# One level of Strassen's scheme in the FFN's first product: seven block products for eight, with the block sums made on the chip

## The chip, the core and the metric

The kernel runs on one core of a Trainium2 chip. Its time is the device time of one execution in microseconds (us). The engines are TensorE (PE; PEld is its weight load), VectorE (DVE), ScalarE (ACT), GpSimd (POOL) and SyncE (SP), whose queue issues nearly all transfers.

## The reference

One step of a backbone of two layers on 640 tokens (512 latent, 128 context) of 1024 features, in fp32. Each layer is an FFN, a mixer of three head groups, and an FFN again. Vectors that shift, scale and gate (`sh`, `sc`, `gt`) come from a conditioning vector by a product with `w_ada`, one set for the context and one for the latent tokens.

```python
def swiglu(x, w_in, w_out):          # w_in 1024 x 5632, w_out 2816 x 1024
    g, u = jnp.split(x @ w_in, 2, axis=-1)
    return (jax.nn.silu(g) * u) @ w_out
...
    u = rmsnorm(h, p["g_norm"][0]) * (1.0 + sc1) + sh1
    h = h + 0.5 * gt1 * swiglu(u, p["w_ff_in"][0], p["w_ff_out"][0])
    u = rmsnorm(h, p["g_norm"][1]) * (1.0 + sc2) + sh2
    y, cache = mix(u, p, lam_init, ctx)
    h = h + gt2 * y
    u = rmsnorm(h, p["g_norm"][2]) * (1.0 + sc3) + sh3
    h = h + 0.5 * gt3 * swiglu(u, p["w_ff_in"][1], p["w_ff_out"][1])
```

## The kernel before

Features lie on the partitions and tokens along them. The tokens are cut into two halves, `HALF`: 384 and 256. An fp32 product is made of three fp32r ones (`mm3`): each operand is a pair H + L, where ScalarE casts H (`split`, L187) and VectorE subtracts it from the fp32 value to give L (L188).

An FFN (`ffn`) has 22 chunks f of 128 hidden features, in three groups of 8, 7 and 7. For each chunk `load1` loads the gate columns and the up columns of `w_ff_in`, 1024 x 128 each, and splits both. `unit1(f, hf)` then multiplies them with the tokens of one half: 2 x 8 x 3 = 48 matmuls into the PSUM tile `gu`. Behind it come tanh on ScalarE and three instructions on VectorE, which give silu(g) * u as a pair for the second product. After a group, `unit2(d, hf)` multiplies all its chunks with 128 columns of `w_ff_out` (PSUM tile `w`), and `update` adds the gated result to the residual `h` on VectorE (L689). `tail` runs the next norm's first half beside the last `unit2` of the second half of the tokens.

The modulation vectors are 72 units, of which 8 are computed in the startup on TensorE. `pump` computes the other 64, one behind each chunk and one behind each column block of the second product, in program order: 32 in the first FFN and 32 in the second, both of layer 0. A unit (`ada_unit`) is a load of 1 MB and 16 multiply-adds of 256 columns on VectorE (`adacc`, L274 and L276), four transposes on TensorE (`adt`) and a reduction (`adred`).

The order of the instructions on each engine is set at build time, from the program order and a model of the engines; on the chip each engine takes its queue in that order. In the startup and in the mixer a planner in the kernel (`Sched`) writes the order, with estimated lengths and due times. The buffers of the FFN's modulation are given back before the mixer begins.

Of the kernel before, what the change touches and what calls it, by code (L numbers as in the profile page):

```python
# [16 lines left out]
P = 128  # L17
D = 1024
# [10 lines left out]
GROUPS = ((0, 8), (8, 15), (15, 22))  # L29
# [5 lines left out]
class Buf:  # L35
    """a buffer of one of the scheduler's pools, held from the operation that allocates it to the last of its users"""
# [9 lines left out]
class Sched:  # L46
    """List scheduler for the mixer: operations with engine, length (ns), dependencies, buffers and deadline (us) are issued in
    the order in which a model of the engines would start them."""
# [33 lines left out]
    def op(self, eng, ns, fn, deps=(), dl=0.0, alloc=(), use=()):  # L82
        """eng: one letter, or several with a length each"""
# [82 lines left out]
class Net:  # L166
    def __init__(self, tc, a, depth=DEPTH):
        self.tc, self.nc, self.a, self.depth = tc, tc.nc, a, depth
        self.n1 = self.n2 = 0
        self.head = None  # L170

# [1 line left out]
    def mm(self, out, lhsT, rhs, start, stop):  # L173
        self.nc.tensor.matmul(out, lhsT, rhs, start=start, stop=stop)  # L174

    def mm3(self, out, sH, sL, mH, mL, start, stop):
        self.mm(out, sH, mH, start, False)
        self.mm(out, sH, mL, False, False)
        self.mm(out, sL, mH, False, stop)

    def split(self, raw, shape):
        """raw (fp32 AP) -> exact fp32r pair"""
        nc = self.nc
        n = int(np.prod(shape[1:]))
        H = self.hlp.tile(shape, F32R, tag="wH", name="wH", bufs=5)
        L = self.hlp.tile(shape, F32R, tag="wL", name="wL", bufs=5)
        nc.scalar.copy(H, raw)  # L187
        nc.vector.tensor_tensor(L, raw, H.bitcast(F32), ALU.subtract)  # L188
        return H, L

# [10 lines left out]
    def rpow(self, out, x):  # L201
        """out = x ** -0.5 (both small fp32 SBUF)"""
# [5 lines left out]
    def consts(self, ctx):  # L208
# [24 lines left out]
            # silu of the conditioning vectors  # L233
# [6 lines left out]
    def mixconsts(self):  # L240
# [5 lines left out]
        # additive masks for the diagonal blocks, [s, t]: fwd keeps s <= t, bwd keeps s >= t  # L246
# [4 lines left out]
        # one-hot columns: a column broadcast over 128 selects a row  # L251
# [47 lines left out]
    def startup(self):  # L299
        """the first modulation vectors, the residual stream to feature-major, its first norm, and the first units of the first FFN"""  # L300
# [1777 lines left out]
```

## Time and profile before

| | |
|---|---|
| median of 3 runs | 2793.17 us (2791.73 to 2793.29) |
| profiled execution | span 2790.0 us from first to last instruction, one core |
| TensorE busy | 2739.9 us, 98% of the span |
| VectorE busy | 1762.5 us, 63% |
| ScalarE busy | 1028.0 us, 37% |
| FFN 1, 2 (layer 0), us from the span's start | 52 to 527, 947 to 1434 |
| FFN 3, 4 (layer 1) | 1434 to 1885, 2312 to 2772 |

Busy is the time in which an engine works on an instruction. Two instructions that overlap on an engine are counted once in its busy time, so the distance between starts, and not the length of one, is what an instruction costs in a row of them. The bounds of the FFNs are read from the chain and rounded.

### The profile page before, as it was taken

Reading aid. Unit: us, or ns where it says so; the run is one execution under the profiler, and the core shown is the slowest. Engines: PE = TensorE matmul, PEld = TensorE weight load, DVE = VectorE, ACT = ScalarE, POOL = GpSimd, SP = SyncE. Lnnn points to the kernel's source line nnn. Section 1 sums busy time; section 2 is a strip of 40 time slices with the busy share of each in tenths; the row PEclk is TensorE's granted clock in tenths of the full one; section 3 lists DMA queues with packets and bytes.
Section 4 is the critical chain, followed back from the end, with each engine's and each line's share of the span. In section 5 each row is a group of like instructions: output and inputs, shape, how many; then the busy total and the mean of one; then the engine's idle time right before and its main releaser. Section 6 shows DMA issues by size and latency. Waiting matters only on the chain.

```text
span 2790.0 us, 46051 instructions
## 1 busy us (share of the span) xinstructions
PE 2739.9 (98%) x18423; PEld 2630.1 (94%) x18423; DVE 1762.5 (63%) x3848; ACT 1028.0 (37%) x2275; POOL 308.8 (11%) x508
## 2 busy tenths in 40 slices
PE   8999999999989999999999999999999999999998
PEld 5999999988889999999999999998888899999998
DVE  5988888666865798788863333338667646333334
ACT  5212222456666421222242122226657644212121
POOL 1000000142522100000000000003343220000000
PEclk9999999999999999999999999999999999999999
DMA  8544454222102354445422222222211033222321
GB/s 264 174 153 142 137 158 134 87 93 88 40 3 77 112 171 137 149 146 152 129 76 76 76 72 80 67 98 81 86 54 31 3 106 83 84 64 69 87 70 52
DMA packets 361933, 276.38 MB, mean 99 GB/s; under 512 B 23720, under 2 KB 349432, under 8 KB 361720
## 3 DMA queue, kind: packets, MB, share of 16 engines
q1 hardware_dynamic: 361720, 273.44, 32.2%
q8 instruction: 145, 2.38, 0.4%
q14 instruction: 68, 0.56, 0.1%
HBM read 259.25 MB, written 14.16 MB: 98 GB/s over the span
## 4 chain that ended last, share of the span: by engine, by line
PE 91%; DVE 3%; ACT 2%; POOL 1%; DMA 1%; issue 1%; SPq 0%; POOLq 0%; DVEq 0%; ACTq 0%
PE gu L174 44%; PE w L174 22%; PE zps L174 6%; PE wo L174 4%; PE tr L965 4%; PE y L174 3%; PE sc L174 2%; PE num L174 2%; PE adt L278 1%; PE z L174 1%; DMA out_new_b_n<-cst 1%; POOL m L1011 1%; PE adp L174 1%; PE st L174 1%; POOL rr L205 0%
## 5 line engine op out<-in xcount | busy, mean ns | idle before, releaser
L174 PE MATMUL gu<-uH,wH 128*128 128x256 f32 (+1 forms) x2816 | 872.4, 310 | 0.0
L174 PE MATMUL gu<-uL,wH 128*128 128x256 f32 (+1 forms) x2816 | 868.9, 309 | 0.1
L174 PE MATMUL gu<-uH,wL 128*128 128x256 f32 (+1 forms) x2816 | 868.6, 309 | 0.0
L174 PEld LDWEIGHTS gu<-uL,wH 128*128 128x128 f32 x2816 | 534.0, 190 | 0.8 <-DVE uL L650 0.4
L174 PEld LDWEIGHTS gu<-uH,wH 128*128 128x128 f32 x2816 | 533.8, 190 | 0.5 <-issue 0.4
L174 PEld LDWEIGHTS gu<-uH,wL 128*128 128x128 f32 x2816 | 533.9, 190 | 0.0
L187 ACT CAST wH<-raw 128x1024 fp32r<-128x1024 f32 (+1 forms) x268 | 274.0, 1022 | 556.7 <-PE w L174 359.1
L174 PE MATMUL w<-hH,wH 128*128 128x384 f32 (+1 forms) x1408 | 435.6, 309 | 0.0
L174 PE MATMUL w<-hH,wL 128*128 128x384 f32 (+1 forms) x1408 | 433.6, 308 | 0.0
L174 PE MATMUL w<-hL,wH 128*128 128x384 f32 (+1 forms) x1408 | 433.0, 308 | 0.0
L188 DVE TENSOR_TENSOR wL<-raw,wH 128x1024 fp32r<-128x1024 f32 (+1 forms) x268 | 319.3, 1193 | 160.1 <-ACT wH L187 159.9
L276 DVE SCALAR_TENSOR_TENSOR adacc<-adaw,cs,adacc 128x256 f32<-128x256 f32 x896 | 385.5, 477 | 2.8
L174 PEld LDWEIGHTS w<-hL,wH 128*128 128x128 f32 x1408 | 264.8, 188 | 0.0
L174 PEld LDWEIGHTS w<-hH,wL 128*128 128x128 f32 x1408 | 264.5, 188 | 0.0
L174 PEld LDWEIGHTS w<-hH,wH 128*128 128x128 f32 x1408 | 264.2, 188 | 0.2 <-DVE o L667 0.2
L689 DVE SCALAR_TENSOR_TENSOR h<-w,mod,h 128x128 f32<-128x128 f32 (+1 forms) x288 | 117.6, 435 | 215.8 <-PE w L174 215.7
L716 ACT ACTIVATE th<-gu 128x256 f32<-128x256 f32 (+1 forms) x173 | 75.2, 434 | 457.5 <-PE gu L174 457.5
L611 POOL TENSOR_TENSOR ssum<-ssum,sq 128x384 f32<-128x384 f32 (+1 forms) x36 | 33.4, 929 | 1899.9 <-ACT sq L610 1886.7
L717 DVE SCALAR_TENSOR_TENSOR th<-th,gu 128x256 f32<-128x256 f32 (+1 forms) x173 | 83.5, 483 | 212.7 <-ACT th L716 212.1
L722 ACT CAST hH<-th 128x256 fp32r<-128x256 f32 (+1 forms) x173 | 79.5, 459 | 251.0 <-DVE th L718 251.0
L174 PE MATMUL zps<-wH,uH 128*128 128x512 f32 x352 | 145.8, 414 | 0.0
L174 PE MATMUL zps<-wH,uL 128*128 128x512 f32 x352 | 139.1, 395 | 0.0
(293 smaller groups left out, 3922.8 us busy)
## 6 DMA issues: line engine op xcount, KB each, us to landing
raw<-in_w_ff_in SPq DMA_DIRECT2D x176, 512.0 KB
adaw<-in_w_ada SPq DMA_DIRECT2D x72, 1024.0 KB
raw<-in_w_ff_out SPq DMA_DIRECT2D x32, 896.0 KB
raw<-in_w_ff_out SPq DMA_DIRECT2D x16, 1024.0 KB
rawi<-in_w_in SPq DMA_DIRECT2D x16, 1024.0 KB
rawo<-in_w_out SPq DMA_DIRECT2D x8, 1024.0 KB
bspill<-z SPq DMA_DIRECT2D x20, 256.0 KB
rawi<-in_w_in SPq DMA_DIRECT2D x8, 512.0 KB
```

What stands on the lines that cost most here:

```text
L174: self.nc.tensor.matmul(out, lhsT, rhs, start=start, stop=stop)
L187: nc.scalar.copy(H, raw)
L188: nc.vector.tensor_tensor(L, raw, H.bitcast(F32), ALU.subtract)
L276: nc.vector.scalar_tensor_tensor(acc, raw[:, k, :], self.cs[:, 8 * v + k : 8 * v + k + 1], acc, ALU.mult, ALU.add)
L278: nc.tensor.transpose(pt[:, (2 * v + j) * P : (2 * v + j + 1) * P], acc[:, j * P : (j + 1) * P], self.ident)
L611: (nc.gpsimd if d in SSG else nc.vector).tensor_tensor(ssum[:, :w], ssum[:, :w], sq[:, :w], ALU.add)
L689: nc.vector.scalar_tensor_tensor(hh, ps[:, s0:s1], gm[:, v, d : d + 1], hh, ALU.mult, ALU.add)
L716: nc.scalar.activation(th[:, :w], ps[:, 0, :w], AF.Tanh, scale=0.5)
L717: nc.vector.scalar_tensor_tensor(th[:, :w], th[:, :w], 1.0, ps[:, 0, :w], ALU.add, ALU.mult)
L722: nc.scalar.copy(H, th[:, :w])
L965: nc.tensor.transpose(pt[:, i * P : (i + 1) * P], x, ident)
L1011: nc.gpsimd.tensor_tensor(m2[:, :, e * hw : (e + 1) * hw], z[:, :, o * hw : (o + 1) * hw], tb[:, 1, e * hw : (e + 1) * hw].unsqueeze(1).to ...
```

## The change

For each chunk the first product is C = A B, where A has two row blocks (gate and up, index s) and two column blocks (the halves of the 1024 features, e), and B has the two halves of the features and two halves of the tokens, now of 320 each (`UH`). Winograd's form of Strassen's scheme makes C of seven block products. On the token side T1 = B12 - B11, T3 = B22 - B12, T2 = B22 - T1 and T4 = B21 - T2 (signs folded into the weights) are made once in each norm (`u_steps`) and held as pairs. On the weight side S1 to S4 are made for each chunk, in the loaded tile, and the seven blocks are split by `split4`. The sums of the products are made partly in PSUM, by going on with an accumulation, and partly on VectorE (`wino`). The last product, which completes the gate of the second token half, is left to the next chunk's pass (`rest`). The first two chunks of an FFN are still computed in the plain way with the new halves (`plain0`, `plain1`).

The groups are four, of 6, 6, 5 and 5 chunks; the second product keeps the old halves and its code otherwise. `pump` is called at the same places: with four groups that makes 36 units in the first FFN and 28 in the second. A modulation unit loads its weights in two halves of 512 KB. In the startup, weights of the modulation have three buffers for five, and GpSimd may make some of the sums; elsewhere `u_steps` runs them on VectorE. Buffers are laid out anew, and four weight pairs are kept for five. The rest of the diff is renaming of buffers and removal of comments.

```diff
-GROUPS = ((0, 8), (8, 15), (15, 22))
+UH = 320
+QK = KD // 2
+GROUPS = ((0, 6), (6, 12), (12, 17), (17, 22))
+UCOMB = dict(B11=(8, 9), B21=(10, 11), B22=(0, 1), T1=(2, 3), T2=(4, 13), T3=(5, 6), T4=(7, 12))
...
+    def split4(self, raw):
+        nc = self.nc
+        i = self.nw8 = (self.nw8 + 1) % 8
+        w = self.wtile("HL"[i % 2], [P, 2, QK, P], i // 2)
+        nc.scalar.copy(w[:, 0], raw)
+        nc.vector.tensor_tensor(w[:, 1], raw, w[:, 0].bitcast(F32), ALU.subtract)
+        return w[:, 0], w[:, 1]
...
+    def ada_unit(self, l, s, u):
         nc, a = self.nc, self.a
         pt = self.ps1("adt")
+        c0 = s * D + u * 256
+        acc = [self.adp.tile([P, 256], F32, tag="adacc", name="adacc", bufs=3) for v in range(2)]
+        for e in range(2):
+            raw = self.adp.tile([P, QK, 256], F32, tag="adaw", name="adaw", bufs=2)
+            nc.sync.dma_start(raw, a["w_ada"][l, e * 512 : (e + 1) * 512, c0 : c0 + 256].rearrange("(k p) c -> p k c", p=P))
+            for v in range(2):
+                for k in range(QK):
+                    col = self.cs[:, 8 * v + 4 * e + k : 8 * v + 4 * e + k + 1]
+                    if e == 0 and k == 0:
+                        nc.vector.tensor_scalar(acc[v], raw[:, 0, :], col, None, ALU.mult)
+                    else:
+                        nc.vector.scalar_tensor_tensor(acc[v], raw[:, k, :], col, acc[v], ALU.mult, ALU.add)
...
-        S = Sched(dict(ps1=4, ps2=2, adaw=5, row=2, nx=2, nu=2, dg=3, w=5, raw=2), strict=("nx", "nu", "dg", "w", "raw"))
+        S = Sched(dict(ps1=4, ps2=2, adaw=3, row=2, nx=2, dg=3, w=4, raw=2), strict=("nx", "dg", "raw"))
...
+    def plain0(self, st, kk, k):
+        B = self.uc["B21" if kk else "B11"]
+        for s in range(2):
+            H, L = st["W"][s]
+            kw = QK * kk + k
+            self.mm3(st["ps"][:, s, :UH], H[:, kw], L[:, kw], B[0][:, k], B[1][:, k], kw == 0, k == QK - 1, True)
...
+    def plain1(self, st, k):
+        T1, B22 = self.uc["T1"], self.uc["B22"]
+        for s in range(2):
+            H, L = st["W"][s]
+            out = st["ps1"][:, s, :UH]
+            self.mm3(out, H[:, k], L[:, k], T1[0][:, k], T1[1][:, k], k == 0, False)
+            self.mm3(out, H[:, QK + k], L[:, QK + k], B22[0][:, k], B22[1][:, k], False, k == QK - 1)
...
+        def t2():
+            th = st["th", hf]
+            nc.vector.scalar_tensor_tensor(th, th, 1.0, g, ALU.add, ALU.mult)
+            nc.vector.tensor_tensor(th, th, u, ALU.mult)
...
+        def xu(d, raw):
+            def x(e):
+                xs[d] = self.npool.tile([P, UH], F32, tag="nx", name="nx", bufs=2)
+                nc.vector.tensor_tensor(xs[d], self.h[d][:, hf * UH : hf * UH + UH], rb, ALU.mult)
+            def u(e):
+                am, bm = self.mod[(l, 3 * i + 1)], self.mod[(l, 3 * i)]
+                r = raw()
+                for v, s0, s1 in segs:
+                    if v == 1 and dve:
+                        nc.vector.tensor_scalar(r[:, s0:s1], xs[d][:, s0:s1], am[:, v, d : d + 1], bm[:, v, d : d + 1], ALU.mult, ALU.add)
+                    else:
+                        nc.scalar.activation(r[:, s0:s1], xs[d][:, s0:s1], AF.Identity, scale=am[:, v, d : d + 1], bias=bm[:, v, d : d + 1])
+            add(("x", d), "D", UH, x)
+            add(("u", d), "A", UH, u, ("x", d))
...
+        def hi(n, k, src, *deps):
+            add(("H" + n, k), "A", UH, lambda e: nc.scalar.copy(uc[n][0][:, k], src()), *deps)
+        def low(n, k, src, *deps):
+            def f(e):
+                if uc[n][1] is None:
+                    self.ut[13] = uc[n][1] = self.utile(13).rearrange("p (k t) -> p k t", k=QK)
+                ve(e).tensor_tensor(uc[n][1][:, k], src(), uc[n][0][:, k].bitcast(F32), ALU.subtract)
+            add(("L" + n, k), "DG", UH, f, *deps)
+        def comb(n, k, dst, a, b, op, *deps):
+            add((n, k), "DG", UH, lambda e: ve(e).tensor_tensor(dst(), a(), b(), op), *deps)
...
+            a, b = (lambda k=k: A[k]), (lambda k=k: B[k])
+            b1, b2 = (lambda k=k: b11[:, k]), (lambda k=k: b21[:, k])
+            xu(k, lambda k=k: new(A, "ua", k))
+            xu(QK + k, lambda k=k: new(B, "ub", k))
+            hi("B22", k, b, ("u", QK + k))
+            low("B22", k, b, ("HB22", k))
+            comb("t3", k, b, b, a, ALU.subtract, ("u", k), ("LB22", k))
+            comb("t1", k, a, a, b1, ALU.subtract, ("t3", k))
+            hi("T1", k, a, ("t1", k))
+            low("T1", k, a, ("HT1", k))
+            hi("T3", k, b, ("t3", k))
+            low("T3", k, b, ("HT3", k))
+            comb("t2", k, b1, b, b1, ALU.add, ("t1", k))
+            comb("t4", k, b2, b2, b1, ALU.subtract, ("t2", k))
+        for k in range(QK):
+            hi("T4", k, lambda k=k: b21[:, k], ("t4", k))
+            low("T4", k, lambda k=k: b21[:, k], ("HT4", k))
+            hi("T2", k, lambda k=k: b11[:, k], ("t2", k))
+        for k in range(QK):
+            low("T2", k, lambda k=k: b11[:, k], ("HT2", k), *(("LT4", z) for z in range(QK)))
...
+            for key, engs, n, fn, deps in self.u_steps(l, i, hf, pb[:, :UH], True, lambda n, k: abt[n][:, k]):
+                fn(engs[0])
...
+        def prod(out, w, name, start):
+            H, L = w
+            uH, uL = self.uc[name]
+            for k in range(QK):
+                self.mm3(out, H[:, k], L[:, k], uH[:, k], uL[:, k], start and k == 0, k == QK - 1, True)
+        def weights(f):
+            raw = load1(f)
+            A11, A12, A21, A22 = (raw[:, s, e * QK : (e + 1) * QK] for s in range(2) for e in range(2))
+            tt = nc.vector.tensor_tensor
+            w = {}
+            w["A11"] = self.split4(A11)
+            tt(A11, A11, A21, ALU.subtract)
+            w["S3"] = self.split4(A11)
+            w["A12"] = self.split4(A12)
+            tt(A11, A22, A11, ALU.subtract)
+            w["S2"] = self.split4(A11)
+            tt(A12, A12, A11, ALU.subtract)
+            w["A22"] = self.split4(A22)
+            tt(A21, A21, A22, ALU.add)
+            w["S1"] = self.split4(A21)
+            w["S4"] = self.split4(A12)
+            return w
+        def rest(st):
+            ps = st["xp"]
+            prod(ps[:, 0, :UH], st["w"]["S4"], "B22", False)
+            st["m"] = (ps[:, 0, :UH], st["m7"])
+            post(st, 1)
+        def wino(f, prev):
+            st = dict(q=f - g0)
+            sc = lambda t, b: self.npool.tile([P, UH], F32, tag=t, name=t, bufs=b)
+            w = st["w"] = weights(f)
+            tt = nc.vector.tensor_tensor
+            xp = st["xp"] = self.ps2("gu")
+            x, p = xp[:, 0, :UH], xp[:, 1, :UH]
+            prod(x, w["A11"], "B11", True)
+            m1 = sc("m1", 1)
+            nc.scalar.copy(m1, x)
+            prod(p, w["S3"], "T3", True)
+            m7 = st["m7"] = sc("m7", 2)
+            nc.scalar.copy(m7, p)
+            if prev is not None:
+                rest(prev)
+            a = self.ps1("ga")[:, :UH]
+            prod(a, w["A12"], "B21", True)
+            tt(m1, m1, a, ALU.add)
+            prod(x, w["S2"], "T2", False)
+            X = sc("X", 1)
+            nc.scalar.copy(X, x)
+            prod(p, w["A22"], "T4", False)
+            tt(X, X, p, ALU.add)
+            st["ps"] = None
+            prod(x, w["S1"], "T1", False)
+            tt(m7, m7, x, ALU.add)
+            st["first"] = (m1, X)
+            post(st, 0)
+            return st
...
+                            if kk == 0:
+                                pl[f]["ps"] = self.ps2("gu")
+                            elif f == 1:
+                                next(self.pend)
+                            for k in range(QK):
...
+            prev = None
             for f in fs:
-                load1(f)
-                for hf in range(2):
-                    unit1(f, hf)
+                prev = wino(f, prev)
                 self.pump(1)
+            rest(prev)
...
-        S.grow("wo", 5)
+        S.grow("wo", 4)
```

## Rows read from the trace of the kernel before

**Rows 1.** The page, part 1: busy us, share of the span, instructions.

```profile
PE 2739.9 (98%) x18423; PEld 2630.1 (94%) x18423; DVE 1762.5 (63%) x3848; ACT 1028.0 (37%) x2275; POOL 308.8 (11%) x508
```

**Rows 2.** The page, part 2: busy tenths in 40 slices.

```profile
PE   8999999999989999999999999999999999999998
...
DVE  5988888666865798788863333338667646333334
```

**Rows 3.** The page, part 4: the chain, by line.

```profile
PE gu L174 44%; PE w L174 22%; PE zps L174 6%; PE wo L174 4%; PE tr L965 4%; PE y L174 3%; PE sc L174 2%; PE num L174 2%; PE adt L278 1%; PE z L174 1%; DMA out_new_b_n<-cst 1%; POOL m L1011 1%; PE adp L174 1%; PE st L174 1%; POOL rr L205 0%
```

**Rows 4.** Windows: the four FFNs; then the start and four passes of FFN 1.

```profile
core 0: us, PE busy (x) PEld busy (x) DVE busy (x) ACT busy (x) POOL busy (x), PEclk, DMA share, GB/s
52.00:527.00 475.00, 475.00 (x3282) 474.82 (x3283) 389.62 (x889) 119.61 (x190) 7.05 (x8) 1.00 0.48 147
947.00:1434.00 487.00, 486.92 (x3360) 486.25 (x3359) 400.08 (x911) 133.79 (x217) 7.00 (x8) 1.00 0.44 135
1434.00:1885.00 451.00, 451.00 (x3083) 451.00 (x3083) 178.39 (x298) 114.61 (x182) 5.53 (x6) 1.00 0.27 80
2312.00:2772.00 460.00, 460.00 (x3142) 459.87 (x3141) 183.16 (x311) 119.22 (x192) 6.13 (x7) 1.00 0.24 69
...
52.00:94.00 42.00, 42.00 (x292) 41.82 (x292) 36.28 (x91) 16.69 (x33) 0.74 (x1) 1.00 0.52 144
108.50:166.50 58.00, 58.00 (x402) 58.00 (x401) 50.69 (x115) 15.32 (x25) 0.00 (x0) 1.00 0.53 168
```

**Rows 5.** Windows, instructions of tile adacc alone: FFN 1, 2 and 3.

```profile
core 0: us, PE busy (x) PEld busy (x) DVE busy (x), PEclk, DMA share, GB/s
52.00:527.00 475.00, 19.39 (x128) 14.67 (x128) 212.28 (x512) 1.00 0.48 147
947.00:1434.00 487.00, 19.34 (x128) 14.67 (x128) 202.04 (x488) 1.00 0.44 135
1434.00:1885.00 451.00, 0.00 (x0) 0.00 (x0) 0.00 (x0) 1.00 0.27 80
```

**Rows 6.** The chain in order of time (start, us, what): passes, second product.

```profile
137.53 14.07 PE gu L174 x96
152.03 14.07 PE gu L174 x96
...
1541.02 55.90 PE w L174 x384
1596.92 98.52 PE gu L174 x672
```

**Rows 7.** Timeline of VectorE, FFN 1 (start, us, instruction, [idle before]).

```profile
start us, us, engine line op out<-in xcount [idle before <-releaser]
...
217.80 2.35 DVE L188 TENSOR_TENSOR wL<-raw,wH 128x1024 fp32r<-128x1024 f32 x2
220.97 0.62 DVE L689 SCALAR_TENSOR_TENSOR h<-w,mod,h 128x384 f32<-128x384 f32 x1 [0.82 <-PE w L174]
223.80 0.61 DVE L689 SCALAR_TENSOR_TENSOR h<-w,mod,h 128x128 f32<-128x128 f32 x2 [2.21 <-PE w L174]
224.32 0.68 DVE L280 TENSOR_REDUCE adred<-adt 128x4 f32<-128x512 f32 x1
...
225.52 5.62 DVE L276 SCALAR_TENSOR_TENSOR adacc<-adaw,cs,adacc 128x256 f32<-128x256 f32 x14
231.06 1.22 DVE L188 TENSOR_TENSOR wL<-raw,wH 128x1024 fp32r<-128x1024 f32 x1
```

**Rows 8.** Timeline of VectorE at the head of FFN 3.

```profile
1425.43 1.01 DVE L650 TENSOR_TENSOR uL<-nu,uH 128x384 fp32r<-128x384 f32 x2
...
1427.30 0.56 DVE L650 TENSOR_TENSOR uL<-nu,uH 128x384 fp32r<-128x384 f32 x1
...
1439.37 0.42 DVE L640 TENSOR_TENSOR nx<-h,nbc 128x256 f32<-128x256 f32 x1 [0.51 <-PE nbc L174]
...
1440.17 0.34 DVE L644 TENSOR_SCALAR nu<-nx,mod,mod 128x128 f32<-128x128 f32 x1
1440.43 0.75 DVE L640 TENSOR_TENSOR nx<-h,nbc 128x256 f32<-128x256 f32 x2
...
1441.42 0.60 DVE L644 TENSOR_SCALAR nu<-nx,mod,mod 128x128 f32<-128x128 f32 x2
```

**Rows 9.** Groups by shape of ScalarE, FFN 3 (busy us, mean ns).

```profile
line engine op names shapes xcount | busy us, mean ns | idle before us <-releasers
L187 ACT CAST wH<-raw 128x1024 fp32r<-128x1024 f32 x47 | 49.3, 1048 | 106.7 <-PE w L174 70.4 <-PE gu L174 36.3
...
L722 ACT CAST hH<-th 128x256 fp32r<-128x256 f32 x22 | 8.9, 406 | 38.8 <-DVE th L718 38.8
```

**Rows 10.** Timeline of TensorE at the head of FFN 3.

```profile
1426.83 0.28 PE L174 MATMUL w<-hH,wL 128*128 128x256 f32 x1
1426.95 0.34 PE L174 MATMUL gu<-uH,wH 128*128 128x384 f32 x1
```

**Rows 11.** Timeline of the SP queue in the startup.

```profile
2.72 1.03 SPq L339 DMA_DIRECT2D adaw<-in_w_ada  x2
...
6.06 5.24 SPq L339 DMA_DIRECT2D adaw<-in_w_ada  x2
11.34 3.52 SPq L346 DMA_DIRECT2D x<-in_x_sample  x1
...
15.38 3.97 SPq L358 DMA_DIRECT2D raw<-in_w_ff_in  x2
```

**Rows 12.** Windows of a mixer (columns as in rows 4).

```profile
724.00:728.00 4.00, 3.82 (x28) 3.28 (x26) 3.34 (x7) 2.64 (x6) 1.07 (x1) 1.00 0.46 144
728.00:732.00 4.00, 2.55 (x12) 1.43 (x11) 3.67 (x9) 3.27 (x11) 3.68 (x5) 1.00 1.02 281
732.00:736.00 4.00, 3.41 (x17) 2.73 (x17) 3.35 (x7) 3.07 (x12) 3.15 (x7) 0.57 0.91 239
736.00:740.00 4.00, 3.62 (x31) 3.04 (x30) 3.63 (x15) 3.20 (x12) 2.32 (x5) 1.00 0.01 3
```

More of the change, by code (lines that the diff above doesn't have):

```diff
@@ new lines, in startup, with pe @@
+        pl = {f: dict(q=f) for f in range(2)}
+        pb = {f: buf("ps2") for f in range(2)}
+        last = {}
+        wof = lambda f: (tuple(x[1] for x in Ws[f]), [y for x in Ws[f] for y in x[2]])
+        for kk in range(2):
+            for f in range(2):
+                wbs, wops = wof(f)
+                nm = "B11" if kk == 0 else "B21"
+                for k in range(QK):
+                    def pe(f=f, kk=kk, k=k):
+                        if kk == 0 and k == 0:
+                            pl[f]["ps"] = self.ps2("gu", pb[f].slot)
+                            pl[f]["W"] = [x[0]["hl"] for x in Ws[f]]
+                        self.plain0(pl[f], kk, k)
+                    us = (*wbs, pb[f])
+                    last[f] = op("P", 6 * 147, pe, (*wops, nop["H" + nm, k], nop["L" + nm, k], last.get(f)), 50 + 4 * kk + f + k * 0.1, (pb[f],) if kk + k == 0 else (), wbs if kk + k == 0 else us)
+                if kk == 0:
+                    last[f] = op("A", 2 * act(UH), lambda f=f: self.plain_copy(pl[f], f), (last[f],), 50, use=(pb[f],))
@@ new lines, in startup, with pe @@
+        for f in range(2):
+            self.post_ops(S, pl[f], 0, (pb[f],), last[f], 60 + f)
+        pb2 = buf("ps2")
+        wbs, wops = wof(0)
+        o = last[0]
+        for k in range(QK):
+            def pe(k=k):
+                if k == 0:
+                    pl[0]["ps1"] = self.ps2("gu", pb2.slot)
+                self.plain1(pl[0], k)
+            o = op("P", 12 * 147, pe, (o, *(nop[x, k] for x in ("HT1", "LT1", "HB22", "LB22"))), 62 + k, (pb2,) if k == 0 else (), wbs if k == 0 else (*wbs, pb2))
@@ L694, in ffn @@
         gm = lambda: self.mod[(l, gs)]
+        self.hid = {} if self.head is None else self.hid
         w1 = a["w_ff_in"][l, j]
@@ L1250, in hi @@
             def hi():
[L1251 to L1252 removed]
+                if wb.slot < 4:
+                    H, L = self.wpair(shape, wb.slot)
+                else:
+                    H, L = (zp.tile(shape, F32R, tag="w5" + x, name="w" + x, bufs=1) for x in "HL")
                 nc.scalar.copy(H, get())
@@ L1276, in mixer @@
         mark = S.n
-        held = [S.hold("w", i) for i in range(4)]
+        held = [S.hold("w", (slot0 + i) % 4) for i in range(4)]
         qh = [S.hold("ps2", i) for i in zslots]
@@ L1921, in wout @@
         W = dict(self.wo_w)
+        self.nw = 3
         def unit(d, hf):
@@ L1947, in open_h @@
         hp = self.h_stack.enter_context(self.pool("hp"))
-        self.h = [[hp.tile([P, c1 - c0], F32, name=f"h{d}_{i}") for i, (c0, c1) in enumerate(HALF)] for d in range(KD)]
+        self.h = [hp.tile([P, T], F32, name=f"h{d}") for d in range(KD)]
     def spill(self, out):
```

438 lines of the change are left out of this document (236 added, 202 removed).

## The prediction

> **What bounds the kernel now.** I read the page's first two parts, then the chain that ended last, then the busy times cut into the four FFNs, then VectorE's order of work inside them. TensorE is busy for 98% of the span and VectorE for 63% [rows 1]. The slices show that the 63% is a mean over two kinds of stretch: VectorE stands at 8 to 9 tenths in slices 2 to 7 and mostly at 8 in slices 14 to 20, the two FFNs of the first layer, and at 3 tenths in slices 22 to 26 and 34 to 39, those of the second [rows 2]. The chain is TensorE nearly throughout; the FFN's first product alone (`gu`) is 44% of it [rows 3]. So TensorE sets the end today, but in the first two FFNs VectorE is close behind: 389.6 of 475 us and 400.1 of 487, against 178.4 of 451 and 183.2 of 460 in the last two [rows 4]. The difference is the modulation: the products `adacc`, 212 and 202 us of VectorE in FFN 1 and 2, none in 3 and 4 [rows 5].
>
> **Prices.** One pass of `unit1` over both halves (96 matmuls of 320 columns on average) takes 14.07 us where nothing else runs: seven of them, 672 matmuls, took 98.52 [rows 6]; with a modulation unit's four transposes it is 14.50 from one pass to the next. On VectorE I take the distance from start to start, not the length, since back-to-back instructions overlap. Two subtractions of 1024 took 2.35 us where one takes 1.22, so the second adds 1.13 [rows 7]; at 384 it adds 1.01 - 0.56 = 0.45, at 256 it adds 0.75 - 0.42 = 0.33 [rows 8]. That is a line of 1.04 ns a column: 0.60 us for 512 columns and 0.40 for 320, the two widths that the change brings and that the trace lacks; the neighbours on both sides hold these to some 0.03. A modulation unit takes VectorE from 224.32 to 231.06, 6.74 us [rows 7].
>
> **TensorE's side.** A `wino` pass has 7 products of 4 x 3 matmuls of 320 columns: 84 for 96, so 84/96 x 14.07 = 12.31 us, a saving of 1.76. Two of 22 chunks stay plain, so 20 x 1.76 = 35.2 us an FFN and 141 in all, if TensorE stays the bound. The second product keeps its matmuls: four groups in place of three, the same 22 chunks at 55.90 / 8 = 6.99 us [rows 6].
>
> **VectorE's side.** Before, a pass has 2 subtractions of 1024 for the weights and 3 instructions on each half of the tokens: 2 x 1.13 + 3 x (0.45 + 0.33) = 4.6 us. After, it has 7 subtractions and 4 block sums of 512, and 3 sums of products and 6 instructions of the activation, all of 320: 11 x 0.60 + 9 x 0.40 = 10.2 us. The pass costs VectorE 5.6 us more. In FFN 3 and 4 that is 10.2 beside 12.31 of TensorE, and TensorE stays last. In FFN 1 and 2 each pass brings a modulation unit as well: 10.2 + 6.7 = 16.9 us of VectorE beside 12.31 + 0.43 = 12.7 of TensorE. There VectorE becomes the bound: 16.9 against the 14.50 that a pass takes now. ScalarE has 7 casts of 512, 3 copies and 4 activations of 320 in a pass, some 8 us by its rows of 1024 and 256 [rows 9], and stays beside.
>
> FFN 1 by VectorE's busy time: 389.6; plus 20 x 5.6 = 112; plus 4 units, since the pump is called 36 times in FFN 1 for 32 (the fourth group adds four), 27; plus the updates of `h` of the fourth group, 8 x (0.62 + 0.61 - 0.16) = 9 [rows 7]; plus the sums and pairs of the first norm, 12 subtractions more and 16 block sums of 320, 11 us, of which I leave 2 to GpSimd, which the startup may use: 9. That is 547 us for a stretch of 475: +72 even without a pause. Pauses there will be at the start (42 us with 36.3 busy today [rows 4]) and behind the last modulation unit, where two of the four column blocks of the last group, 5 x 6.99 / 2 = 17.5 us of TensorE, need VectorE for about half: 6 + 8 us. Waits inside the passes I take at 1%, 5 us. FFN 1: **+91**.
>
> FFN 2: 400.1 + 112 - 27 (28 units are left) + 9 + 11 (its norm, on VectorE alone) = 505 for 487: +18 without a pause. The units run out in the third group, so the fourth is TensorE's again: 5 x 12.31 + 5 x 6.99 = 96.5 us, in which VectorE has some 80 of work; 16 us of pause, 8 more while the norm waits for its statistics, and 4 of waits: **+46**.
>
> FFN 3 and 4: -35.2 each. Against it stands the norm of the second token half. Before, TensorE covers it: the first `gu` started at 1427, the second half's `nx` at 1439.4, and 256 columns of one feature tile cost VectorE some 0.9 us [rows 8, 10]. After, one k of the second half costs 2 products, 3 subtractions, 4 block sums and two modulations of 128 columns, about 4 us, so 16 for four k's, and `plain1`, which needs T1 and B22 of each, has 1.75 us of TensorE a k. With 14 us of `plain0` ahead of it and 7 of `plain1` to spread, about 8 us of TensorE are not covered (bounds: 0, and 16 if nothing covers). I add 3 us for passes where VectorE is late (bounds 0 and 20). FFN 3 and 4: **-24 each**. The mixers, `wout` and the last norm keep their work; five weight buffers become four in `wout`, where TensorE has 7 us of matmuls a buffer: 0. The startup has three buffers for its modulation weights and not five; the SP queue now waits for a buffer ahead of the loads behind it, the tokens and the first weights among them, and two such loads took 5.24 us to issue [rows 11]: bounds 0 and 10, I take +3.
>
> Sum: 91 + 46 - 48 + 3 = +92. The profiled execution has a span of 2790.0, and the median of the runs is 2793.17, 3.2 above: 2882 + 3 = **2885 us**.
>
> The Trainium skill speaks against this change too: "VectorE: DVE Perf Modes", section "Mode 2x_2P", says that an fp32 sum of two tensors can't use the second read port and stays at one element a cycle, so each block sum is paid in full. The trace agrees in kind, with 1.04 ns a column. By the page's 0.96 GHz alone, an estimate, 512 columns would be 0.53 us and 320 columns 0.33, a pass 8.9 for 10.2, and the sum 52 us lower, 2833; the rows have an overhead of 0.07 us an instruction on top, and they decide.
>
> **The rivals.** *A. VectorE never pauses and TensorE's saving in the second layer comes in full:* 72 + 18 - 70 + 3 = +23, 2816 us. For it: VectorE ran without a gap for stretches of several us in FFN 1 [rows 7], and the modulation can fill waits. Against it: the last stretch of each FFN has no modulation left.
>
> *B, the other side: TensorE stays the bound in all FFNs.* If the modulation's products found room elsewhere, the gain would be 141 less the two 8 us at the norms and some waits: about 2680. The point from which it decides is 12.7 us of VectorE a pass in FFN 1; it has 16.9. The products stay on VectorE and in the same FFNs, and before the mixer their buffers are given back, so they can't slip into it. Short of that, rival A with all of VectorE's time in FFN 1 and 2 5% lower would give 2816 - 53 = 2763. Against it: my prices reproduce VectorE's 389.6 in FFN 1: 32 x 6.74 + 20 x 4.6 = 308, and the 24 weight splits (1.0 to 1.1 us) and 24 updates (1.07) of the second product add 50; the first chunks and the next norm remain. 4 in 100.
>
> *C. VectorE and TensorE wait for each other by turns.* In a `wino` pass each product waits for a pair whose sum is on VectorE, and the sums of products on VectorE wait for TensorE; both queues are in order, so behind one such wait stand the pairs of the next chunk. If a tenth of VectorE's time goes that way, FFN 1 pays 54 and FFN 2 42 beyond the pauses, and FFN 3 and 4 lose their gain (27 more each): 72 + 14 + 54 + 18 + 24 + 42 + 3 = +227, about 3020. For it: 7 splits in a row alternate between ScalarE and VectorE. Against it: one pass of pairs is buffered ahead, and today VectorE is 87% busy in such passes (50.69 of 58) without TensorE waiting [rows 4].
>
> *D. TensorE's clock.* In the mixer, after 4 us with 2.55 busy, the granted clock was 0.57 in the next 4 [rows 12]: part of that time at the lower level, 1.2 GHz. In FFN 1 TensorE would idle 4 us a pass. If it ran at the lower level for 4 us of each, a pass would need 2 us more, 14.7, still under 16.9; only at the lower level throughout, 24.6 a pass, would it decide: 40 x 7.7 = 308 us more, about 3190. 3 in 100. The Trainium skill, "TensorE: Matmul & The Clock Gate", section "HAM oscillation", warns of such alternation of work and waits; the rows show it for idle stretches alone.
>
> **How the numbers follow.** The forecast, VectorE as the bound of FFN 1 and 2 with few waits, between 2825 and 2945: 72 in 100. A: 8, B: 4, C: 13, D: 3. The range 2810 to 2960 leaves out B, D, most of C above and half of A. A measurement of this kernel can tell 0.2%, 5.6 us, from no change. Faster: B and a little of A, 0.05; within 0.2%: 0.03; slower: 0.92.
>
> **What would show it.** Right: in FFN 1 VectorE busy for 95% or more and `gu` waiting for VectorE's `wL` or its sums; passes of 16.5 to 17.5 us there, and of 12.3 to 12.8 in FFN 3 and 4; 560 us for FFN 1 and 530 for FFN 2; a gap of some 8 us at the head of FFN 3 and 4. Wrong: if subtractions of 512 take under 0.5 us, if modulation units no longer stand in FFN 1's passes, or if passes in FFN 3 are over 13.5 us, where the waits of C would be the reason.

## The result and the profile after

The change makes the kernel slower: 2973.46 us (median of 4 runs, 2971.2 to 2977.85) against 2793.15, a ratio of 1.065 (95% interval 1.0635 to 1.0665). The prediction was 2885, in a range of 2810 to 2960: the direction held, the size was half of what came, and the time lies 13 us above the range.

The page of the changed kernel, parts 1, 2 and 4:

```profile
PE 2753.1 (93%) x17469; PEld 2549.7 (86%) x17469; DVE 2295.3 (77%) x5054; ACT 1304.2 (44%) x3011; POOL 326.5 (11%) x521
...
PE   7898988889998998989899999999999999999999
...
DVE  5999999887676779989996857766767665866765
...
PE 73%; DVE 18%; ACT 4%; issue 2%; DMA 2%; POOL 1%; SPq 0%; DVEq 0%; POOLq 0%; ACTq 0%
```

TensorE, at 98% before [rows 1], is at 93%, and VectorE stands at 8 to 9 tenths through most of both FFNs of layer 0. The chain gives it 18%. Windows of the four FFNs:

```profile
core 0: us, PE busy (x) PEld busy (x) DVE busy (x) ACT busy (x) POOL busy (x), PEclk, DMA share, GB/s
52.00:649.00 597.00, 509.40 (x3060) 471.97 (x3058) 553.15 (x1257) 190.90 (x383) 22.36 (x22) 0.93 0.42 123
1071.00:1623.00 552.00, 496.21 (x3099) 463.83 (x3097) 500.98 (x1133) 198.79 (x393) 8.55 (x8) 0.96 0.38 113
1623.00:2077.00 454.00, 440.86 (x2919) 429.70 (x2918) 319.44 (x621) 192.50 (x379) 6.47 (x7) 0.99 0.28 82
2504.00:2971.00 467.00, 451.37 (x3016) 438.85 (x3014) 328.83 (x642) 195.57 (x385) 8.03 (x10) 0.99 0.27 77
```

Beside [rows 4]: VectorE has 553 us of work in FFN 1, where 547 were forecast, and 501 in FFN 2 for 505. Its work was sized rightly; its idle time was not: 44 us and 51, where 19 and 28 stood in the sum.

I cut every profiled execution at the same points, the first matmul of `gu` in an FFN and the first of a mixer (`z`). Stretches in us; the last three columns are experiments told below:

| stretch | before | after | foreseen difference | measured | new layout, plain products | the same, no modulation products | scheme, no modulation products |
|---|---|---|---|---|---|---|---|
| startup and FFN 1 | 529.0 | 649.3 | +94 | +120.3 | 574.4 | 554.0 | 527.0 |
| mixer 1 | 418.2 | 425.6 | 0 | +7.4 | 423.8 | 424.8 | 426.2 |
| FFN 2 | 479.7 | 547.7 | +46 | +67.9 | 517.4 | 497.9 | 466.8 |
| FFN 3 | 466.0 | 460.1 | -24 | -5.9 | 490.3 | 493.5 | 460.8 |
| mixer 2 | 418.6 | 424.4 | 0 | +5.8 | 424.1 | 424.0 | 422.7 |
| FFN 4 and end | 478.3 | 464.1 | -24 | -14.2 | 497.0 | 496.7 | 466.1 |
| span | 2790.0 | 2971.3 | +92 | +181.3 | 2927.0 | 2890.9 | 2769.6 |

A pass with a modulation unit in FFN 1, VectorE's timeline from one `m` of line 959 to the next:

```profile
284.39 0.49 DVE L959 TENSOR_TENSOR m<-m,gu 128x320 f32<-128x320 f32 x1
284.80 3.65 DVE L316 SCALAR_TENSOR_TENSOR adacc<-adaw,cs,adacc 128x256 f32<-128x256 f32 x9
...
292.55 0.68 DVE L917 TENSOR_TENSOR raw<-raw 128x512 f32<-128x512 f32 x1
293.16 0.68 DVE L921 TENSOR_TENSOR raw<-raw 128x512 f32<-128x512 f32 x1
...
296.65 0.48 DVE L951 TENSOR_TENSOR m<-m,ga 128x320 f32<-128x320 f32 x1
297.05 0.49 DVE L640 TENSOR_TENSOR th<-th,m 128x320 f32<-128x320 f32 x1
...
302.02 0.49 DVE L959 TENSOR_TENSOR m<-m,gu 128x320 f32<-128x320 f32 x1
```

17.63 us, with 17.3 of VectorE's work and nearly without a gap, where 16.9 was forecast. Not every pass is like this one; the next part shows another kind. The starts of two sums of 512 columns are 0.61 apart and of two of 320 columns 0.40: the two prices that the trace of before lacked, 0.60 and 0.40, hold.

**Where VectorE pauses.** Its largest waits in FFN 1, behind the startup:

```profile
engine line waited for: us in total, times, longest us
DVE wH L211 <- ACT wH L210: 13.5, 6, 2.7
DVE h L879 <- PE w L181: 6.0, 7, 1.5
DVE wL L211 <- ACT wL L210: 5.0, 2, 2.7
```

18.5 us go to the casts of ScalarE, an engine that is busy for 173 of these 570 us. Seven of the eight waits are 2.4 to 2.7 us long, 18.0 together. The timelines of VectorE and of ScalarE around one such wait:

```profile
589.05 0.68 DVE L211 TENSOR_TENSOR wH<-raw,wH 128x512 fp32r<-128x512 f32 x1
592.36 0.69 DVE L211 TENSOR_TENSOR wH<-raw,wH 128x512 fp32r<-128x512 f32 x1 [2.63 <-ACT wH L210]
```

```profile
587.96 0.62 ACT L210 CAST wH<-raw 128x512 fp32r<-128x512 f32 x1 [0.98 <-DVE raw L917]
591.38 0.43 ACT L946 COPY m<-gu 128x320 f32<-128x320 f32 x1 [2.81 <-PE gu L181]
591.71 0.62 ACT L210 CAST wH<-raw 128x512 fp32r<-128x512 f32 x1
```

ScalarE's queue is in order, and the copy of the second product out of PSUM (line 946) stands ahead of the next cast. It waits 2.81 us for TensorE; the cast stands behind it, and VectorE, the bound, behind the cast. All seven long waits, and two more in FFN 2, stand behind this copy.

Why TensorE is late shows in the granted clock. Windows of the pass above and of the pass with this wait, then TensorE and the copy in the pass above, and TensorE in the pass with the wait:

```profile
284.40:302.00 17.60, 14.21 (x88) 12.74 (x88) 17.32 (x38) 6.72 (x14) 0.00 (x0) 1.00 0.32 105
578.90:599.30 20.40, 17.05 (x88) 15.44 (x88) 17.47 (x40) 6.91 (x14) 0.00 (x0) 0.83 0.28 84
```

```profile
292.40 1.63 PE L181 MATMUL gu<-u,wL 128*128 128x320 f32 x10
293.87 1.19 PE L181 MATMUL ga<-u,wH 128*128 128x320 f32 x7
```

```profile
294.07 0.43 ACT L946 COPY m<-gu 128x320 f32<-128x320 f32 x1 [0.18 <-PE gu L181]
```

```profile
588.52 2.82 PE L181 MATMUL gu<-u,wH 128*128 128x320 f32 x10
591.18 1.18 PE L181 MATMUL ga<-u,wL 128*128 128x320 f32 x7
```

The ten matmuls ahead of the copy take 2.66 us from first start to the next group's (588.52 to 591.18), where they take 1.47 in the pass above: part of this pass ran at the lower of TensorE's two levels, 1.2 GHz for 2.4. Where the clock stays at 1.00 the same copy waits 0.18 us, and no cast is late. Sixteen passes of FFN 1 follow another in their group. The seven with a long wait take 20.4 us, the first of them 22.7, at a granted clock of 0.78 to 0.83; the other nine take 15.3 to 17.7, at 1.00. What TensorE did ahead of the fall does not tell them apart: it was busy for 2.27 of the 4 us from 580, and for 2.38 of the 4 us from 284, where the clock stayed. So this is the turn-taking of rival C, set off by the clock of rival D, in seven of sixteen passes and at 2.8 us each. Why the clock falls in these passes and not in the others is not shown.

**Where TensorE pauses in FFN 3 and 4.** The head of FFN 4, timelines of VectorE and of TensorE, and the window of the stretch:

```profile
2517.84 0.16 DVE L696 TENSOR_SCALAR ms<-nst 128x2 f32<-128x2 f32 x1 [3.20 <-PE nst L181]
...
2521.46 0.48 DVE L728 TENSOR_TENSOR nx<-h,nbc 128x320 f32<-128x320 f32 x1
...
2541.50 1.70 DVE L749 TENSOR_TENSOR u<-hid,u 128x320 fp32r<-128x320 f32 x4
```

```profile
2507.16 0.46 PE L181 MATMUL gu<-u,wH 128*128 128x320 f32 x2
...
2524.43 0.31 PE L181 MATMUL gu<-u,wL 128*128 128x320 f32 x1
2526.77 0.41 PE L181 MATMUL gu<-u,wH 128*128 128x320 f32 x1 [2.03 <-ACT u L743]
```

```profile
2524.00:2547.00 23.00, 16.17 (x90) 14.14 (x89) 22.84 (x59) 14.15 (x32) 0.00 (x0) 0.93 0.00 1
```

Windows of the head of FFN 3 and of FFN 4, from the first `gu` on:

```profile
1622.00:1660.00 38.00, 26.57 (x145) 23.90 (x146) 30.39 (x78) 22.73 (x52) 1.66 (x2) 0.91 0.20 55
2507.00:2547.00 40.00, 31.74 (x193) 28.97 (x192) 34.05 (x86) 23.53 (x53) 0.71 (x1) 0.96 0.15 42
```

At 0.147 us each, these matmuls are 21 and 28 us of work: TensorE lost some 17 us in the first head and 12 in the second. The second half's norm keeps VectorE from 2521.46 to 2543.20, 21.7 us (I had 16), and it starts 14.3 us after the first `gu`, because its statistics come that late (in FFN 3, 18.5 us). The plain products of the first half are over at 2524.7: 3 us of cover were left of the 14 that I had counted. Then TensorE goes at VectorE's pace: 90 matmuls in 23 us, where 156 of 0.147 us fit. Before, the list of TensorE's waits is empty in this stretch.

### The profile page after: what moved, and what is told of

The parts are those of the page before. It is cut to its first block, busy times and chain, and to the rows that moved or that the text cites. A ratio compares the mean times of both kernels' runs of the same rounds, so it can differ in the third digit from the quotient of the medians.

```text
span 2971.3 us, 46414 instructions
## 1 busy us (share of the span) xinstructions
PE 2753.1 (93%) x17469; PEld 2549.7 (86%) x17469; DVE 2295.3 (77%) x5054; ACT 1304.2 (44%) x3011; POOL 326.5 (11%) x521
## 4 chain that ended last, share of the span: by engine, by line
PE 73%; DVE 18%; ACT 4%; issue 2%; DMA 2%; POOL 1%; SPq 0%; DVEq 0%; POOLq 0%; ACTq 0%
PE gu L181 27%; PE w L181 18%; PE zps L181 5%; DVE adacc L316 5%; PE ga L181 4%; PE tr L1218 3%; PE wo L181 3%; PE y L181 3%; PE sc L181 2%; PE num L181 2%; DVE u L749 1%; PE z L181 1%; DVE wH L211 1%; DVE wL L211 1%; DVE wL L202 1%
## 5 line engine op out<-in xcount | busy, mean ns | idle before, releaser
L181 PE MATMUL gu<-u,wH 128*128 128x320 f32 x3392 | 624.2, 323 | 66.6 <-ACT u L743 17.0
L181 PE MATMUL w<-hid,wH 128*128 128x256 f32 (+1 forms) x2816 | 622.6, 312 | 5.2 <-ACT wH L201 2.5
L181 PEld LDWEIGHTS gu<-u,wH 128*128 128x128 f32 x3392 | 532.8, 195 | 106.0 <-ACT u L743 20.1
L181 PE MATMUL gu<-u,wL 128*128 128x320 f32 x3136 | 572.4, 319 | 44.2 <-DVE m L959 10.0
L181 PEld LDWEIGHTS gu<-u,wL 128*128 128x128 f32 x3136 | 489.0, 193 | 75.1 <-DVE m L959 14.4
L181 PEld LDWEIGHTS w<-hid,wH 128*128 128x128 f32 x2816 | 477.5, 191 | 9.6 <-ACT wH L201 3.6
L181 PE MATMUL w<-hid,wL 128*128 128x256 f32 (+1 forms) x1408 | 436.3, 314 | 7.8 <-DVE wL L202 7.7
L181 PEld LDWEIGHTS w<-hid,wL 128*128 128x128 f32 x1408 | 267.7, 191 | 11.3 <-DVE wL L202 11.3
L181 PE MATMUL zps<-wH,u 128*128 128x512 f32 x704 | 243.3, 406 | 1.8 <-ACT u L836 1.7
L211 DVE TENSOR_TENSOR wL<-raw,wL 128x512 fp32r<-128x512 f32 x280 | 191.6, 687 | 35.1 <-ACT wL L210 34.3
```

What stands on the lines that cost most here:

```text
L211: nc.vector.tensor_tensor(w[:, 1], raw, w[:, 0].bitcast(F32), ALU.subtract)
```

## The experiments

Each time is the median of one to ten executions (one in runs 1, 2 and 4). The kernel before, measured beside them, took 2792.2 to 2793.2 us.

**1. The scheme without the modulation's products.** In `ada_unit` the `scalar_tensor_tensor` of the other seven k is left out:

```diff
-                    else:
-                        nc.vector.scalar_tensor_tensor(acc[v], raw[:, k, :], col, acc[v], ALU.mult, ALU.add)
```

> The changed kernel, with the 14 multiply-adds of each modulation unit in FFN 1 and 2 left out (their loads, first products, transposes and reductions stay; the vectors are then not those of the reference). Theory V (VectorE's own work bounds FFN 1 and 2): a pass in FFN 1 falls from 17.6 us to TensorE's 12.7, FFN 1 from 597 to about 475 and FFN 2 from 548 to about 465, the whole to about 2765. Theory W (VectorE and TensorE wait for each other by turns, whatever VectorE's load): passes stay above 14.5 us and the whole above 2850.

Measured: 2771.4 us, 202 below the changed kernel, all of it in FFN 1 and 2 (table). VectorE is what bounds them.

**2. VectorE's load alone, on the kernel before.** The subtraction of each weight split is written three and four times, so that a pass has seven of 1024 columns for two:

```diff
-        nc.vector.tensor_tensor(L, raw, H.bitcast(F32), ALU.subtract)
+        for _ in range(again):
+            nc.vector.tensor_tensor(L, raw, H.bitcast(F32), ALU.subtract)
...
+            W[f] = [self.split(raw[:, s], [P, KD, P], 3 + s) for s in range(2)]
```

> The kernel before, with VectorE's subtraction of the weights written 7 times a pass for 2 (the same values again), 5.65 us more of VectorE a pass: the change's load without its products. V: FFN 3 and 4 as before, FFN 1 and 2 longer by what 22 x 5.65 = 124 us leave after their pauses, 40 us each and some waits: 2880 to 2930. W (the order of the seven products makes the waits, and load alone doesn't): FFN 1 and 2 no longer than their VectorE sum, under 2870.

Measured: 2913.2 us. 5 x 1.13 = 5.65 us a pass, the scheme's 5.6, cost 49 us in FFN 1, 56 in FFN 2 and 17 in FFN 3 and 4 together, without one product changed. So a part of the result needs nothing of the scheme but its VectorE time.

**3. The units spread over the four FFNs**, 24, 18, 18 and 4 for 36 and 28:

```diff
-            x = next(self.adaq, None)
-            if x is not None:
-                self.ada_unit(*x)
+            if self.calls in self.when:
+                self.ada_unit(*next(self.adaq))
+            self.calls += 1
```

> The changed kernel with the 64 modulation units spread over the four FFNs, 24, 18, 18 and 4 for 36, 28, 0 and 0, each still in time for its first use. V: 12 and 10 units of 6.74 us leave FFN 1 and 2, -81 and -67 us; FFN 3 has room for most of its 18 (319 + 121 of VectorE in some 460) and grows by 10 to 20: about 2840. W: a unit costs the same wherever it stands, about 2970.

Measured: 2815.95 us, ratio 1.0084 (1.0054 to 1.0113). The same work, 22 of the 64 units of it moved to where VectorE is idle, gives back 157 of the 180 us; FFN 2 falls to 472.3, FFN 3 rises to 468.8. It is the best version found that computes everything, and it doesn't beat the kernel before.

**4. The weight sums on GpSimd:**

```diff
-            tt = nc.vector.tensor_tensor
+            tt = nc.gpsimd.tensor_tensor
```

> The changed kernel with the four block sums of the weights of each chunk on GpSimd. V, if GpSimd works beside VectorE: 2.4 us less of VectorE a pass, 40 passes in FFN 1 and 2, about 2880. Rival: GpSimd and VectorE hold each other up (in the startup a VectorE sum of 320 took 1.05 us for 0.49 while GpSimd worked); then the 4 x 1.2 us of GpSimd a pass cost VectorE as much as they take from it or more: 2970 to 3070.

Measured: 3123.9 us, beyond both. Weight splits on VectorE in FFN 4 (min, median and max of one in ns), in the changed kernel:

```profile
L211 DVE TENSOR_TENSOR wH<-raw,wH x70: 681/687/696, 2544.3 to 2910.2; 128x512 fp32r<-128x512 f32 x70
```

and with the sums on GpSimd, with GpSimd's own, and a moment of both timelines:

```profile
L211 DVE TENSOR_TENSOR wH<-raw,wH x62: 678/693/1789, 2659.4 to 3056.3; 128x512 fp32r<-128x512 f32 x62
```

```profile
L914 POOL TENSOR_TENSOR raw<-raw x18: 1282/1473/1626, 2660.2 to 3048.7; 128x512 f32<-128x512 f32 x18
```

```profile
2663.78 1.47 POOL L917 TENSOR_TENSOR raw<-raw 128x512 f32<-128x512 f32 x1 [0.63 <-DVE wL L211]
```

```profile
2664.03 1.77 DVE L211 TENSOR_TENSOR wH<-raw,wH 128x512 fp32r<-128x512 f32 x1
```

A split takes 0.69 us alone and up to 1.8 where a GpSimd sum runs, and the sum takes twice VectorE's time. The Trainium skill, "SBUF — State Buffer", section "SBUF: two separate sides", says that a VectorE instruction with two SBUF inputs and a GpSimd instruction that reads SBUF exclude each other for the whole instruction. The rows agree: the split of 1.77 started 0.25 us behind a sum of 1.47, and 1.77 - 0.69 = 1.08 is near the 1.22 that were left of that sum. Windows of FFN 1 and FFN 4 show where the time went:

```profile
52.00:648.00 596.00, 494.88 (x3063) 459.17 (x3061) 565.20 (x1176) 192.27 (x383) 148.76 (x102) 0.96 0.41 124
2593.00:3122.00 529.00, 471.85 (x2993) 452.78 (x2991) 333.07 (x557) 191.25 (x382) 123.60 (x89) 0.96 0.23 67
```

In FFN 1 VectorE is busy for 565 us, 12 more than with the sums on it, and startup and FFN 1 are as long as in the changed kernel (648.8 for 649.3). The loss is in FFN 2, 3 and 4: 23, 67 and 65 us. In FFN 4 VectorE has 333 us of work in 529, so there it is not VectorE's load that costs but what waits for the slower sums; that part was not tried by itself.

**5. Another order in the heads**, ahead of FFN 2, 3 and 4: T3 and the sums for T2 and T4 behind T1 and B22 of all four k.

```diff
+        if dve:
+            for k in range(QK):
+                late(k)
...
```

> The changed kernel with one order changed: in the norm of the second token half, ahead of FFN 2, 3 and 4, the pair T3 and the sums for T2 and T4 come after T1 and B22 of all four k, which the plain products wait for, and not between them. If the heads are lost because VectorE and ScalarE deliver T1 and B22 too late: some 5 us of VectorE's sums and four ScalarE copies leave the way, so 4 to 10 us less in the heads of FFN 3 and 4 each and 0 to 5 in FFN 2, where VectorE is the bound anyway: 2950 to 2965. Rival, the heads are lost to something else (the products' own waits for PSUM, the clock): 2971 to 2976.

Measured: 2984.0 us, 1.0685 (1.0665 to 1.0705): no gain, rather a loss of 3 us each in FFN 3 and 4 and 10 in FFN 2. In FFN 2 seven passes took 20.4 us or more, at the lower clock for a part, where the changed kernel has two: that is more than the loss there. The order isn't what costs in the heads of FFN 3 and 4.

**6. The modulation on TensorE**, its weights as 16 stationary tiles of 128 x 128 against two columns:

```diff
+        for j in range(2):
+            for k in range(KD):
+                self.mm(pt[:, 2 * j : 2 * j + 2], raws[k // QK][:, k % QK, j * P : (j + 1) * P], self.cs2[:, k], k == 0, k == KD - 1)
```

> The changed kernel with the products of the modulation units on TensorE: the weights of a unit as 16 stationary tiles of 128x128 against two columns, no multiply-adds on VectorE, no transposes. VectorE as the bound of FFN 1 and 2: the time falls well under 2973. How far depends on a price that no trace shows: 16 weight loads of 0.10 to 0.19 us are 1.6 to 3.0 us a unit for 0.35 of the transposes now, for 60 units 75 to 160 us on top of the 2771 without any products: 2845 to 2930. Rival, the waits between the engines rule whoever does the units: within 10 us of 2973.

Measured: 3073.8 us; both expectations fell. Timeline of TensorE, then windows of 4 us:

```profile
300.52 3.95 PE L181 MATMUL adt<-cs,adaw 128*128 128x2 f32 x32
```

```profile
300.00:304.00 4.00, 4.00 (x36) 4.00 (x34) 1.65 (x4) 2.17 (x5) 0.00 (x0) 0.96 0.11 26
304.00:308.00 4.00, 4.00 (x17) 4.00 (x17) 1.96 (x4) 0.62 (x1) 0.00 (x0) 0.50 0.80 238
308.00:312.00 4.00, 4.00 (x21) 4.00 (x21) 3.11 (x6) 0.46 (x1) 0.00 (x0) 0.69 0.07 25
312.00:316.00 4.00, 4.00 (x29) 3.88 (x28) 1.87 (x3) 1.89 (x5) 0.00 (x0) 1.00 0.05 4
```

A unit is 32 matmuls in the trace and 3.95 us, above the 1.6 to 3.0 expected; and in the 4 us behind it the granted clock is 0.50, TensorE's lower level, though it was busy throughout. 17 matmuls pass there, where 29 do at 1.00.

**7. Spread units and the other order in the heads together.**

> The modulation units spread over the four FFNs (24, 18, 18, 4), and the order of the norm's sums as in the run before last. TensorE is then the bound nearly everywhere, and what is saved at the heads of FFN 2, 3 and 4 counts: 3 times 4 to 10 us under the 2816 of the spread alone: 2786 to 2804, level with the kernel before or a little under. Rival, the heads are not a matter of this order: 2813 to 2819.

Measured: 2821.35 us, 1.0104 (1.0089 to 1.012), level with the spread alone at best: the order isn't it here either.

**8. The heads' low parts written twice:**

```diff
+                for _ in range(2 if dve and hf else 1):
+                    ve(e).tensor_tensor(uc[n][1][:, k], src(), uc[n][0][:, k].bitcast(F32), ALU.subtract)
```

> The changed kernel with a suspected cost of the heads doubled: each low part of the second token half (20 subtractions of 320 columns in the norm ahead of FFN 2, 3 and 4) is written twice, 20 x 0.40 = 8 us of VectorE a head. If VectorE's amount of work in the head sets when TensorE goes on there: 8 us in each of three heads, 2973 + 24 = 2997 (2990 to 3003). Rival, TensorE's two plain chunks cover part of it and only FFN 2, where VectorE is the bound throughout, pays: 2978 to 2985.

Measured: 2995.8 us, 1.0724 (1.0706 to 1.0742); 7.6 us more in FFN 3, 7.9 in FFN 4. 8 us of VectorE in a head are 8 us of the time: nothing covers them. FFN 2 is 17 us longer; six of its passes took 20.4 us or more, for two. FFN 1 has no edit, and its instructions have the same order on each engine; it was 7 us shorter, with four passes of 20.4 us at a clock of 0.83 for seven. So the time of a stretch that VectorE bounds varies by 2.8 us with each such pass.

**9. Seven buffers for the seven split weights, and not eight** (`% 7`):

> The changed kernel with a ring of seven buffers for the seven split weights of a pass and not eight. If the waits of VectorE behind ScalarE's casts (28.5 us in FFN 1 and 2 together) come from the ring, whose oldest buffer is free only when TensorE has read it, then they grow: 1 to 3 us in each of 40 passes of FFN 1 and 2, and TensorE waits in FFN 3 and 4 as well: 3010 to 3120. Rival, these casts wait for something else: within 10 us of 2973.

Measured: 2969.1 us. My theory of the ring fell: VectorE's waits for casts did not grow (four long ones in FFN 1, for seven). What they wait for is the copy in ScalarE's queue, as the timeline above shows.

**10. The new layout without the scheme.** All chunks by plain products, with the four groups, the buffers, the startup and the heads of the changed kernel:

```diff
-                prev = wino(f, prev)
+                plain(f)
...
-            rest(prev)
```

> The new layout without the scheme: all 22 chunks by the eight plain block products (12 x 8 = 96 matmuls of 320 columns, 14.07 us), with the four groups, the new buffers, the startup and the heads with their sums of the changed kernel. VectorE has 5.5 us a pass, 12.2 with a unit, and TensorE 14.5, so TensorE is the bound. By the sizes of my prediction the layout costs 3 at the startup and 8 in each of three heads, 2793 + 27 = 2820. By the traces it costs some 14 at the startup, 12 to 20 in each of three heads and 13 in the two mixers: 2793 + 63 to 87 = 2856 to 2880.

Measured: 2928.75 us, 1.049 (1.0474 to 1.0505): the layout alone costs 136, more than either number. (A plain chunk's second product is made in two parts that VectorE adds, as in the first two chunks of the changed kernel.)

**11. One part of the layout on the kernel before**: modulation weights in two halves, two buffers of half the size.

```diff
-                self.ada_unit(*x, self.ada_load(*x, self.adp, 2))
+                self.ada_unit(*x)
```

> The kernel before with one part of the new layout: a modulation unit's weights come in two halves of four k, in two buffers of 4 KB a partition, where they came whole, in two of 8 KB. My prediction gave this no cost outside the startup: 2793 (2788 to 2798). Rival: a half's buffer is free only when VectorE has used it, so the next load comes late; in the new layout with plain products VectorE waited 77 us for these loads. Where VectorE is busy for 85% of FFN 1 and 2, a part of that comes out in TensorE's time: 2805 to 2830.

Measured: 2795.3 us, 1.001 (1.000 to 1.002). This part costs next to nothing there; the rival fell.

**12. The layout with plain products, without the modulation's.** The edits of 10 and 1 together.

> The new layout with plain products, and the 14 multiply-adds of each modulation unit left out. If what the layout costs in FFN 1 and 2 beyond FFN 3 and 4 (83 us for 43) comes from the modulation, its late loads and VectorE's waits, it goes: 2929 - 30 to 45 = 2884 to 2899. Rival, it comes from the startup and the norm in the head alone: 2919 to 2932.

Measured: 2894.0 us. Of the layout's 136 us 35 came with the modulation's products in FFN 1 and 2. Whether through their load on VectorE or through its 77 us of waits for their weights in run 10 is not told apart. The other 101 are there without them: 25, 18, 27 and 18 in the four FFNs and 12 in the mixers.

Runs 1, 10, 12 and the changed kernel make a square. Where VectorE has room, the scheme takes 2894 to 2771, 123 us less; where it also has the modulation, 2929 to 2973, 45 more.

## Why the prediction was right and wrong

- **VectorE becomes the bound of FFN 1 and 2: right.** Runs 1, 2 and 3 show it from three sides. The busy times (553 for 547, 501 for 505) came as worked out, and so did the pass where nothing disturbs it (17.6 for 16.9). Rival B, TensorE as the bound everywhere, fell; so did A, VectorE without pauses.
- **TensorE's saving of 35.2 us an FFN: nearly right.** Between runs 12 and 1 the scheme saves 27, 31, 33 and 31. The chain in order of time has passes in FFN 4 that begin 12.5 us apart, 12.31 forecast:

```profile
2660.09 5.42 PE gu L181 x36
...
2672.56 10.72 PE gu L181 x72
...
2685.04 7.19 PE gu L181 x48
```

- **"Waits inside the passes I take at 1%": this step failed.** 5 and 4 us were set aside; VectorE's idle time in FFN 1 and 2 exceeded the sum's by 25 and 23. In FFN 1 seven passes at the lower clock for a part are 2.8 us longer each, some 20 us. Rival D had this case, at "2 us more, 14.7, still under 16.9", and so at nothing. It compared totals of a pass. But VectorE waits for one product in the middle of the pass, through a copy in ScalarE's queue, and what TensorE has to spare later in the pass does not help there. Rival C's price, a tenth of VectorE's time (54 and 42 us), was too high: what VectorE waited is about half of it, and FFN 3 and 4 kept their passes. I had set ScalarE aside for its busy time ("some 8 us", it "stays beside"); its order is what passes TensorE's delay on. In FFN 2 the largest waits are 15.5 us for TensorE's second product and 10 for casts, of which two such passes are 5:

```profile
DVE h L879 <- PE w L181: 15.5, 16, 2.1
...
DVE wL L211 <- ACT wL L210: 6.1, 5, 2.5
DVE wH L211 <- ACT wH L210: 4.2, 4, 2.5
```

- **"About 8 us of TensorE are not covered": this step failed too.** I costed the second half's norm at 16 us and covered it with 14 of plain products. The norm is 21.7: the sum has 3 subtractions for a k, and there are 5, 20 in all (run 8), so 8 of 0.40 us were missing; four instructions of the plain chunks' activation stand among them. And it starts when 3 of the 14 are left, since the statistics of that half come late. TensorE lost 17 and 12 us in the heads of FFN 3 and 4, at and near my upper bound of 16. What the whole layout costs there in run 12 is 27 and 18 us (its share in FFN 2 and 3 is exact to some 4 us, since the cut between them moves with the last updates). In FFN 2 it is 18 again, where I had put 8 for the wait for the statistics. Run 8 shows that nothing covers the head; runs 5 and 7 tried one other order of the same work, and it did not help.
- **The mixers at 0: wrong by 13 us.** Of the 7.4 in the first, 2.1 are there by the first matmul of `gps` (29.1 us after the first `z` before, 31.2 after), 1.8 more at the first `sc` behind the last `zps` (211.3 and 215.2), and the rest comes between the last `y` and the first matmuls of `wo`. That fewer buffers of weights and of the norm do this was not tried.
- **The startup at +3, bounds 0 and 10: too low.** At 79 us TensorE had begun 102 matmuls of `gu` of 320 columns, some 15 us, and before 193, 97 of 384 and 96 of 256 columns, some 28. In run 12 startup and FFN 1 are 25 us over the kernel before; since VectorE bounds FFN 1 in the changed kernel, it doesn't appear there as a sum of its own.

So the 89 us that the forecast missed are 26 in FFN 1, of which the clock's seven passes are some 20; 22 in FFN 2, where VectorE waits and the head is dearer, not told apart by these runs; 18 and 10 in FFN 3 and 4, of which 9 and 4 are the head beyond its 8 and the rest is not located; and 13 in the mixers.

Two small slips of the prediction change nothing: slice 34 of [rows 2] stands at 6 tenths and not at 3, and the sum of rival C leaves out the 6 us by which FFN 3 and 4 would be longer.

## What to carry to other kernels

Before products are taken from the engine that is the bound, add up the other engines' work in each stage, not over the span: here VectorE had room in half of the kernel and none in the other half, and moving 22 of 64 units of work from one to the other was worth 157 us. Work that makes an operand must be covered by products that don't need it, and the cover counts from the moment at which the inputs are there. An engine with little to do can still hold up the bound, if something that waits stands in its queue ahead of what the bound needs. Through such a queue a delay of an engine that has time to spare, here TensorE at its lower clock, reaches the bound in full.

## What was not expected of the hardware

In FFN 1 passes of the same 84 block matmuls, with TensorE busy for about 2.3 of 4 us in the same part of each, kept a granted clock of 1.00 or fell to 0.83; the same instructions in the same order fell in seven passes in one profile and in four in another (the changed kernel and run 8). TensorE, busy for the whole of a 4 us stretch with matmuls of two columns, had the lower clock in the next 4 (0.50, run 6): being busy did not keep the clock. An fp32 sum of 512 columns on GpSimd takes 1.47 us for VectorE's 0.69 and stretches VectorE's own instructions to 1.8 (run 4), so that taking four sums a pass off VectorE left it with more busy time in FFN 1 and not less.
